# Hybrid decoder layer: attention products in one array shape, split values, a longer lag, and the FFN's token sums on VectorE

## The chip, the core and the metric

The kernel runs on one core of a Trainium2 chip. The metric is the device time of one execution in microseconds (us). The core's engines are named as the profile names them: PE (TensorE's matmuls), PEld (its weight loads), DVE (VectorE), ACT (ScalarE), POOL (GpSimd) and SP, which issues the transfers. Each engine takes its instructions in a fixed order, and they wait for each other through semaphores.

## What is computed

One layer, 512 tokens, width 1024, float32. Three groups of heads share one input projection: six attention heads of 64 channels, a state-space mixer (SSD) and a pooling mixer. Their outputs are joined, projected and added to the input; a gated feed-forward part (FFN) and a last norm follow. Attention selects three blocks of 256 keys, but with 512 tokens there are only two blocks, so it is plain causal attention:

```python
h = rmsnorm(x, norm_mix)
q, k, v, z, xbc, dt_raw, p_in = jnp.split(h @ w_in, offsets, axis=-1)
p = softmax(q @ k.T * 64 ** -0.5 + causal)        # per head, 512 tokens
y_attn = p @ v
y_ssd = ssd_mixer(xbc, z, dt_raw, ...)            # chunks of 128 tokens, gated norm
y_pool = pool_mixer(p_in, pool_w, pool_scale)
x = x + concatenate([y_attn, y_ssd, y_pool]) @ w_out
gate, up = split(rmsnorm(x, norm_ffn) @ w_gate_up)
x = x + (silu(gate) * up) @ w_down
out = rmsnorm(x, norm_final)
```

## The kernel before

**Precision.** Large products are done in float32r on split operands: a value is a high part (rounded by ACT, `AF.Copy` into a float32r tile) and a low part (value minus high part, on DVE or POOL). `mm3` (lines 163 to 168) makes three products of them: high by high, high by low, low by high. Plain float32 products appear too; the trace shows each of those as two rows on PE.

**Stages.** First come the projections: `proj_nat` makes token-major tiles (`pn`: v, and z with dt), `proj_ch` channel-major ones (`pc`: q, k, the conv inputs, the pool input). While they run, small jobs are woven in: attention, SSD, pooling. Then the output projection (`po`, in two halves of columns), then the boundary: each of four token tiles gets its residual (`add_x1`), its norm (`h2_norm`, tile `xh`), a transposition (`h2_bank`, tile `ps_h`) and its split into `h2_hi` and `h2_lo`. The FFN multiplies by a seven-product (Strassen-like) scheme, so it needs sums and differences of token tiles as well: `h2_sums` makes t1 to t4 for token tiles 2 and 3, splits each, and writes them to `T2`, `T3`, `T4` and `h2`. Then the gate and up products (`psf`) and the down products (`pd`, `pdl`).

**Attention.** `evac_v` writes v (`v_sb`, float32). `evac_q` and `evac_k` make, for each pair of heads j (three pairs), `qa` and `qb`: in the own 64 partitions the high part of q, in the other 64 the low part; `ka` and `kb`: the high part of k in both; `kl`: the low parts of both heads, 64 partitions each, made on POOL. `scores` (576 to 593) then needs two products for 128 tokens of queries: q by k over all 128 partitions, and high q by low k over the head's own 64 (line 584). DVE adds the mask and takes the row minimum (589), ACT takes the exponential and its sum (590), DVE the reciprocal (591) and the scaling (592). `probs_t` (595) transposes the probabilities on PE and copies them to SBUF, on ACT for the first head of a pair and DVE for the second. `values` (609 to 614) multiplies v by them in float32, into 64 of the 128 output partitions:

```python
nc.tensor.matmul(ps_o[hd, i * P : (i + 1) * P], v_sb[:, b, col], pt[:, b * P : (b + 1) * P], ...)
```

A step is one head and one tile i of 128 queries, 24 in all, in the order pair, tile, head. `attention_lane` gives out scores of step n, transposes of step n-1, values of step n-2.

**What sets the order.** Lanes (generators) are resumed by a clock that counts the PE time given out so far (`L.tick`, `L.clock`), with delays in the tables `ATT`, `SSD` and marks such as `mark("dt", 9.0)`. A scheduler then places each engine's instructions by its own model when the program is built. `ENG` (line 48) says for token tiles 2 and 3 which of five subtractions of `h2_sums` go to DVE (v) and to POOL (g): in order t3, and the low parts of t2, t3, t1 and t4.

## Time and profile before

| | us |
|---|---|
| median of 3 runs (lowest to highest) | 597.58 (596.22 to 598.58) |
| the profiled execution | 597.45 |
| its span, from the first to the last instruction | 595.7 |
| PE busy | 576.7 (97%) |
| DVE busy | 458.1 (77%) |
| ACT busy | 272.9 (46%) |
| POOL busy | 65.3 (11%) |
| granted TensorE clock, mean of the span | 0.99 |

PE's busy time counts overlapping matmuls once, and the end of a matmul is modelled, so what a matmul costs its neighbours is read from the start of one row to the start of the next. The clock is given as a share of the higher of its two levels (2.4 GHz): 1.00 is that level, 0.50 the lower one (1.2 GHz).

### The profile page before, as it was taken

Reading aid. Unit: us, or ns where it says so; the run is one execution under the profiler, and the core shown is the slowest. Engines: PE = TensorE matmul, PEld = TensorE weight load, DVE = VectorE, ACT = ScalarE, POOL = GpSimd, SP = SyncE. Lnnn points to the kernel's source line nnn. Section 1 sums busy time; section 2 is a strip of 40 time slices with the busy share of each in tenths; the row PEclk is TensorE's granted clock in tenths of the full one; section 3 lists DMA queues with packets and bytes.
Section 4 is the critical chain, followed back from the end, with each engine's and each line's share of the span. In section 5 each row is a group of like instructions: output and inputs, shape, how many; then the busy total and the mean of one; then the engine's idle time right before and its main releaser. Section 6 shows DMA issues by size and latency. Waiting matters only on the chain.

```text
span 595.7 us, 9142 instructions
## 1 busy us (share of the span) xinstructions
PE 576.7 (97%) x3540; PEld 505.9 (85%) x3540; DVE 458.1 (77%) x815; ACT 272.9 (46%) x459; POOL 65.3 (11%) x78
## 2 busy tenths in 40 slices
PE   8998999999999999799999999999999999999994
PEld 5995698777876787799889988999899989999984
DVE  4487558596897757999999987798869977888445
ACT  5674434664553546536525541554144523325135
POOL 5020000201953010500000000000000000000024
PEclk9998999999999999899999999999999999999998
DMA  7952124221221450033623431243224424212003
GB/s 240 308 171 72 35 72 141 96 102 56 70 72 36 137 216 2 36 109 110 206 72 108 146 103 70 77 173 107 70 72 142 139 75 142 72 53 90 2 0 142
DMA packets 19520, 61.64 MB, mean 103 GB/s; under 512 B 2300, under 2 KB 3476, under 8 KB 19476
## 3 DMA queue, kind: packets, MB, share of 16 engines
q1 hardware_dynamic: 19476, 61.05, 30.7%
q8 instruction: 28, 0.46, 0.3%
q14 instruction: 16, 0.13, 0.1%
HBM read 58.93 MB, written 2.11 MB: 102 GB/s over the span
## 4 chain that ended last, share of the span: by engine, by line
PE 89%; DVE 6%; ACT 2%; issue 1%; DMA 1%; SPq 0%; DVEq 0%; ACTq 0%
PE psf L164 11%; PE psf L165 11%; PE psf L166 11%; PE pd L164 6%; PE pd L165 6%; PE pd L166 6%; PE pc L164 5%; PE pc L165 4%; PE pc L166 4%; PE po L164 2%; PE po L165 2%; PE po L166 2%; PE ps_ao L613 2%; PE pn L164 2%; PE pn L166 2%; PE pn L165 2%
## 5 line engine op out<-in xcount | busy, mean ns | idle before, releaser
L165 PE MATMUL pd<-dl,aTh 128*128 128x512 f32 x160 | 63.3, 395 | 0.0
L164 PE MATMUL pd<-dh,aTh 128*128 128x512 f32 x160 | 62.6, 395 | 0.0
L166 PE MATMUL pd<-dh,aTl 128*128 128x512 f32 x160 | 60.0, 395 | 0.0
L1032 DVE TENSOR_TENSOR E<-psf,E 128x256 f32<-128x256 f32 x110 | 42.1, 418 | 11.2 <-PE psf L166 10.3
L164 PE MATMUL psf<-h_hi,gh 128*128 128x256 f32 x176 | 49.9, 285 | 0.1
L165 PE MATMUL psf<-h_lo,gh 128*128 128x256 f32 x176 | 49.7, 283 | 0.0
L165 PE MATMUL psf<-h_lo,sh 128*128 128x256 f32 x176 | 49.7, 282 | 0.0
L166 PE MATMUL psf<-h_hi,gl 128*128 128x256 f32 x176 | 49.7, 283 | 0.0
L166 PE MATMUL psf<-h_hi,sl 128*128 128x256 f32 x176 | 49.5, 281 | 0.0
L164 PE MATMUL psf<-h_hi,sh 128*128 128x256 f32 x176 | 49.5, 281 | 0.0
L136 DVE TENSOR_TENSOR wlo<-raw,whi 128x1024 fp32r<-128x1024 f32 (+3 forms) x29 | 33.2, 1144 | 18.8 <-ACT whi L135 16.1
L135 ACT ACTIVATE whi<-raw 128x1024 fp32r<-128x1024 f32 (+3 forms) x34 | 31.6, 932 | 34.1 <-PE pc L165 19.2
L164 PE MATMUL pc<-hT_hi,whi 128*128 128x512 f32 x104 | 43.2, 415 | 0.0
L165 PE MATMUL pc<-hT_lo,whi 128*128 128x512 f32 x104 | 41.5, 399 | 0.0
L166 PE MATMUL pc<-hT_hi,wlo 128*128 128x512 f32 x104 | 41.4, 398 | 0.0
L1124 POOL TENSOR_TENSOR x<-x,gf 128x512 f32<-128x512 f32 x4 | 5.1, 1299 | 322.6 <-ACT sqf L747 322.6
L782 ACT ACTIVATE dh<-r_d 128x1024 fp32r<-128x1024 f32 x22 | 23.0, 1055 | 33.8 <-PE psf L165 22.5
L782 ACT ACTIVATE sh<-sb 128x1024 fp32r<-128x1024 f32 x22 | 23.2, 1057 | 32.8 <-PE pd L165 26.0
L783 DVE TENSOR_TENSOR sl<-sb,sh 128x1024 fp32r<-128x1024 f32 x22 | 28.0, 1271 | 13.3 <-ACT sh L782 9.6
L166 PEld LDWEIGHTS pd<-dh,aTl 128*128 128x128 f32 x160 | 30.1, 188 | 7.2
L739 DVE TENSOR_TENSOR x<-pd,x 128x512 f32<-128x512 f32 x44 | 28.3, 685 | 10.1 <-PE pd L166 10.1
L164 PEld LDWEIGHTS pd<-dh,aTh 128*128 128x128 f32 x160 | 30.1, 188 | 7.0
(286 smaller groups left out, 1706.3 us busy)
## 6 DMA issues: line engine op xcount, KB each, us to landing
r_g<-wgu SPq DMA_DIRECT2D x22, 512.0 KB, 3.8
r_u<-wgu SPq DMA_DIRECT2D x22, 512.0 KB, 4.1
r_d<-wd SPq DMA_DIRECT2D x22, 512.0 KB, 3.3
raw<-w SPq DMA_DIRECT2D x13, 512.0 KB, 3.3
raw<-wo SPq DMA_DIRECT2D x8, 512.0 KB, 3.2
rawx<-xT SPq DMA_DIRECT2D x8, 256.0 KB, 3.5
rawn<-xn SPq DMA_DIRECT2D x4, 512.0 KB, 4.7
x<-xn SPq DMA_DIRECT2D x4, 512.0 KB, 6.6
```

What stands on the lines that cost most here:

```text
L135: nc.scalar.activation(hi[:, sl], raw[:, sl], AF.Copy)
L136: eng.tensor_tensor(lo[:, sl], raw[:, sl], hi[:, sl].bitcast(F32), ALU.subtract)
L164: nc.tensor.matmul(ps, s_hi, m_hi, start=first, stop=False)
L165: nc.tensor.matmul(ps, s_hi, m_lo, start=False, stop=False)
L166: nc.tensor.matmul(ps, s_lo, m_hi, start=False, stop=last)
L613: nc.tensor.matmul(ps_o[hd, i * P : (i + 1) * P], v_sb[:, b, col], pt[:, b * P : (b + 1) * P], start=(b == 0), stop=(b == i))
L739: nc.vector.tensor_tensor(x1[t][:, cs], ps, x1[t][:, cs], ALU.add)
L782: nc.scalar.activation(hi, src, AF.Copy)
L783: eng.tensor_tensor(lo, src, hi.bitcast(F32), ALU.subtract)
L1032: nc.vector.tensor_tensor(o_, a_, b_, ALU.add)
L1124: nc.gpsimd.tensor_tensor(x1[t][:, :512], x1[t][:, :512], gf[0][:, :512], ALU.mult)
```

## The change

Attention: `evac_v` now splits v into a high part (ACT) and a low part (DVE), side by side in one tile of 128 columns for each head (`v_hl`). The low part of k gets one tile for each head, with zeros in the other 64 partitions (set once on POOL), so that both score products run over 128 partitions. `probs_t` splits the transposed probabilities into `ph` (ACT) and `pl` (DVE) for two query tiles in one tile of 256 columns. `values` multiplies `v_hl` by `ph` and by `pl` in float32r, for two query tiles at a time: the output has the products with the high part of v in one half of the partitions and those with the low part in the other. `attention_out` copies one half across (ACT), adds the halves (DVE), and splits the sum after the second head. The steps now run pair, head, tile; transposes follow their scores by two steps, and values their transposes by two more. The delays of two lanes are longer. `ENG` sends all five subtractions of both token tiles to DVE. The smaller scratch for dynamic DMA frees memory.

```diff
--- before.py
+++ after.py
@@ -41,11 +41,13 @@
 VFIRST = (1, 2, 2, 3)
 WARM = 10
 ATT = (1.2, 0.4, 0.4)
+ATT_LAG = 2
+VAL_LAG = 2
 SSD = (3.0, 3.0, 1.5)
 LAST = 256
 NDEC = 4
 NW = 6
-ENG = ("vggvg", "vvgvg")
+ENG = ("vvvvv", "vvvvv")
 MIX_ORDER = (0, 6, 1, 7, 3, 4, 5, 2)
@@ -270,7 +272,7 @@
         rstd_bc = mp.tile([P, S], F32, name="rstd_bc")
         def norm_lane():
-            yield 20.0
+            yield 23.0
             ps = bank("ps_rstd")
             for t in range(NT):
                 nc.tensor.matmul(ps[:, t * P : (t + 1) * P], rstd[:, t : t + 1].to_broadcast([P, P]), ident, start=True, stop=True)
@@ -347,7 +349,7 @@
             nc.vector.scalar_tensor_tensor(sz[:, t], th, 1.0, sz[:, t], ALU.add, ALU.mult)
             if t == NT - 1:
                 softplus()
-                mark("dt", 9.0)
+                mark("dt", 13.0)
         def softplus():
             nc.scalar.activation(s_, dtr, AF.Abs)
@@ -536,11 +538,17 @@
-        v_sb = mp.tile([P, NT, 384], F32, name="v_sb")
+        v_hl = mp.tile([P, NT, NH, P], F32R, name="v_hl")
+        kl_sb = [mp.tile([P, S], F32R, name=f"kl{h}") for h in range(2)]
         qk_sb = {}
         def evac_v(t, ps):
-            nc.vector.tensor_scalar_mul(v_sb[:, t], ps[:, :384], rstd[:, t : t + 1])
+            src, hi, lo = h3(ps[:, :384]), v_hl[:, t, :, :64], v_hl[:, t, :, 64:]
+            nc.scalar.activation(hi, src, AF.Copy, scale=rstd[:, t : t + 1])
+            nc.vector.scalar_tensor_tensor(lo, src, rstd[:, t : t + 1], hi.bitcast(F32), ALU.mult, ALU.subtract)
             if t == NT - 1:
                 mark("v", 4.0)
@@ -564,9 +572,10 @@
             def f(ps):
                 k = w2k(f"k{j}")
                 nc.vector.tensor_tensor(k, ps, rstd_bc, ALU.mult)
-                kl = qk_tile("kl", j)
-                for name, own, other in (("ka", H0, H1), ("kb", H1, H0)):
+                for name, kl, own, other in (("ka", kl_sb[0], H0, H1), ("kb", kl_sb[1], H1, H0)):
                     t_ = qk_tile(name, j)
+                    if j == 0:
+                        nc.gpsimd.memset(kl[other].bitcast(F32), 0.0)
                     nc.scalar.activation(t_[own], k[own], AF.Copy)
                     nc.scalar.activation(t_[other], k[own], AF.Copy)
                     nc.gpsimd.tensor_tensor(kl[own], k[own], t_[own].bitcast(F32), ALU.subtract)
@@ -575,13 +584,12 @@
         def scores(j, i, h):
             n = (i + 1) * P
-            hd = (H0, H1)[h]
             nm = f"{j}{i}{h}"
             ps = bank(f"ps_s{nm}")
-            q, k, kl = qk_sb["qa" if h == 0 else "qb", j], qk_sb["ka" if h == 0 else "kb", j], qk_sb["kl", j]
+            q, k, kl = qk_sb["qa" if h == 0 else "qb", j], qk_sb["ka" if h == 0 else "kb", j], kl_sb[h]
             qs = slice(i * P, (i + 1) * P)
             nc.tensor.matmul(ps[:, :n], q[:, qs], k[:, :n], start=True, stop=False)
-            nc.tensor.matmul(ps[:, :n], q[hd, qs], kl[hd, :n], start=False, stop=True)
+            nc.tensor.matmul(ps[:, :n], q[:, qs], kl[:, :n], start=False, stop=True)
             L.clock += 2 * max(0.109, n * 0.00042)
             pr = w2k(f"pr{nm}")
             mn = tiny.tile([P, 1], F32, name=f"mn{nm}", tag="mn")
@@ -592,46 +600,65 @@
             nc.vector.tensor_scalar_mul(pr[:, :n], pr[:, :n], sm)
             return pr
-        def probs_t(j, i, h, pr):
+        def probs_t(j, i, h, pr, pt):
             n = (i + 1) * P
             nm = f"{j}{i}{h}"
             ps_t = bank(f"ps_t{nm}")
             for b in range(i + 1):
                 nc.tensor.transpose(ps_t[:, b * P : (b + 1) * P], pr[:, b * P : (b + 1) * P], ident)
             L.clock += 0.11 * (i + 1)
-            pt = w2k(f"pt{nm}")
-            if h == 0:
-                nc.scalar.copy(pt[:, :n], ps_t[:, :n])
-            else:
-                nc.vector.tensor_copy(pt[:, :n], ps_t[:, :n])
-            return pt
+            hi, lo = (x_[:, : i + 1, (i % 2) * P : (i % 2 + 1) * P] for x_ in pt)
+            src = ps_t[:, :n].rearrange("p (b q) -> p b q", q=P)
+            nc.scalar.activation(hi, src, AF.Copy)
+            nc.vector.tensor_tensor(lo, src, hi.bitcast(F32), ALU.subtract)
         def values(j, i, h, pt, ps_o):
-            hd = slice(64 * h, 64 * h + 64)
-            col = slice(128 * j + 64 * h, 128 * j + 64 * h + 64)
             for b in range(i + 1):
-                nc.tensor.matmul(ps_o[hd, i * P : (i + 1) * P], v_sb[:, b, col], pt[:, b * P : (b + 1) * P], start=(b == 0), stop=(b == i))
-            L.clock += 0.22 * (i + 1)
+                q0 = P if b == i else 0
+                w_ = v_hl[:, b, 2 * j + h]
+                o_ = ps_o[:, (i - 1) * P + q0 : (i + 1) * P]
+                for x_ in pt:
+                    nc.tensor.matmul(o_, w_, x_[:, b, q0:], start=(b == 0 and x_ is pt[0]), stop=(b == i and x_ is pt[1]))
+                    L.clock += 0.109 if b < i else 0.07
+        def attention_out(j, h, ps_o, y):
+            own, other = (H0, H1) if h == 0 else (H1, H0)
+            aux = w2k(f"aux{j}{h}")
+            nc.scalar.copy(aux[own], ps_o[other])
+            nc.vector.tensor_tensor(y[own], ps_o[own], aux[own], ALU.add)
+            if h == 1:
+                nc.scalar.activation(mixT_hi[:, j], y, AF.Copy)
+                nc.vector.tensor_tensor(mixT_lo[:, j], y, mixT_hi[:, j].bitcast(F32), ALU.subtract)
+                mark(f"mix{j}", 3.5)
         def attention_lane():
-            steps = [(j, i, h) for j in range(3) for i in range(NT) for h in range(2)]
-            pr, pt, outs = {}, {}, {}
-            for n in range(len(steps) + 2):
+            steps = [(j, i, h) for j in range(3) for h in range(2) for i in range(NT)]
+            pr, pt, outs, ys = {}, {}, {}, {}
+            for n in range(len(steps) + ATT_LAG + VAL_LAG):
                 if n < len(steps):
-                    if steps[n][1:] == (0, 0):
-                        yield when("v", f"k{steps[n][0]}")
-                    pr[n] = scores(*steps[n])
+                    j, i, h = steps[n]
+                    if (i, h) == (0, 0):
+                        yield when("v", f"k{j}")
+                    pr[n] = scores(j, i, h)
                     yield ATT[0]
-                if 1 <= n <= len(steps):
-                    pt[n - 1] = probs_t(*steps[n - 1], pr.pop(n - 1))
+                m = n - ATT_LAG
+                if 0 <= m < len(steps):
+                    j, i, h = steps[m]
+                    if i % 2 == 0:
+                        pt[j, h, i // 2] = [wk.tile([P, NT, 256], F32R, name=f"p{x_}{j}{h}{i}", tag=f"p{x_}") for x_ in "hl"]
+                    probs_t(j, i, h, pr.pop(m), pt[j, h, i // 2])
                     yield ATT[1]
-                if n >= 2:
-                    j, i, h = steps[n - 2]
-                    if (i, h) == (0, 0):
-                        outs[j] = bank(f"ps_ao{j}")
-                    values(j, i, h, pt.pop(n - 2), outs[j])
-                    if (i, h) == (NT - 1, 1):
-                        mix_out(j, outs.pop(j))
+                m -= VAL_LAG
+                if m >= 0 and steps[m][1] % 2:
+                    j, i, h = steps[m]
+                    if i == 1:
+                        outs[j, h] = bank(f"ps_ao{j}{h}")
+                    values(j, i, h, pt.pop((j, h, i // 2)), outs[j, h])
+                    if i == 3:
+                        if h == 0:
+                            ys[j] = w2k(f"y{j}")
+                        attention_out(j, h, outs.pop((j, h)), ys[j])
                     yield ATT[2]
@@ -1211,7 +1238,7 @@
     import concourse.bacc as bacc
     from concourse.bass_utils import run_bass_kernel_spmd as run
-    nc = bacc.Bacc("TRN2", target_bir_lowering=False, num_devices=1)
+    nc = bacc.Bacc("TRN2", target_bir_lowering=False, num_devices=1, dynamic_dma_scratch_size=1024)
     arrays, args = {}, []
     for name, a in pack(inputs).items():
         a = np.ascontiguousarray(a)
```

On PE, at the first steps of attention (`ps_s` scores, `ps_t` transposes, `ps_ao` values, `pc` a projection), there stands before:

```order
L166 MATMUL pc_506<-hT_hi,wlo_361 128x512
L600 MATMUL ps_t_529<-ident,pr_482 128x128
L583 MATMUL ps_s_536<-ka_440,qa_431 128x256
L584 MATMUL ps_s_536<-kl_439,qa_431 128x256
L600 MATMUL ps_t_552<-ident,pr_516 128x128
L613 MATMUL ps_ao_559<-pt_531,v_sb 64x128
L164 MATMUL pc_578<-hT_hi,whi_396 128x512
```

The transpose of the second step's probabilities (`pr_516`) stands right behind the scores of the third. In the changed kernel the first step's transpose stands so:

```order
L168 MATMUL pc_513<-hT_hi,wlo_363 128x512
L608 MATMUL ps_t_554<-ident,pr_489 128x128
L591 MATMUL ps_s_561<-ka_445,qa_437 128x512
L592 MATMUL ps_s_561<-kl_243,qa_437 128x512
L166 MATMUL pc_591<-hT_hi,whi_392 128x512
```

The fourth step's scores (512 columns) stand behind it, where the second step's transpose stood. That one (`pr_523`) comes after the 24 rows of projection `pc_591`, again on PE:

```order
L168 MATMUL pc_591<-hT_hi,wlo_393 128x512
L608 MATMUL ps_t_595<-ident,pr_523 128x128 x2
L591 MATMUL ps_s_603<-kb_450,qb_440 128x128
L592 MATMUL ps_s_603<-kl_244,qb_440 128x128
L489 MATMUL ps_bn_613<-ident,bc_234 128x128 x4
L608 MATMUL ps_t_627<-ident,pr_539 128x128 x3
```

The first values have moved behind the fourth step's transposes.

On PE, at the end of attention, the transposes of the SSD output (`ps_sn`) stand behind this in the changed kernel (`ps_t_1939` is the last step's transpose, `po` the output projection):

```order
L608 MATMUL ps_t_1939<-ident,pr_1862 128x128 x4
L622 MATMUL ps_ao_1949<-ph_1850,v_hl 128x256
L622 MATMUL ps_ao_1949<-pl_1851,v_hl 128x256
L622 MATMUL ps_ao_1949<-ph_1850,v_hl 128x128
L622 MATMUL ps_ao_1949<-pl_1851,v_hl 128x128
L168 MATMUL po_0_1788<-whi_1463,mixT_lo 128x512
L168 MATMUL po_1_1789<-whi_1463,mixT_lo 128x512
L168 MATMUL po_2_1790<-whi_1463,mixT_lo 128x512
L168 MATMUL po_3_1791<-whi_1463,mixT_lo 128x512
L533 MATMUL ps_sn_1991<-ident,sz 128x128
L533 MATMUL ps_sn_1998<-ident,sz 128x128
```

Between the last SSD product (`ps_y`) and the first of these `ps_sn` rows PE now has 13 rows of `po`, 10 transposes, two scores of 512 columns, one pool product (two rows of 512 columns) and 11 value products; before, the first `ps_sn` came behind much more of `po` and of the values.

On DVE, at the boundary, between the sums of token tile 2 and the norm of token tile 3 (`xh`), there stands before:

```order
L947 SCALAR_TENSOR_TENSOR tf_2315<-tf_2313,h2f_2223 128x512
L936 TENSOR_TENSOR h_lo<-tf_2312,h_hi 128x4x128
L759 TENSOR_SCALAR rsaa_2331<-rsay_2330,rsav_2328 128x1
L760 TENSOR_SCALAR rsay_2330<-rsaa_2331,rsay_2330 128x1
L905 SCALAR_TENSOR_TENSOR xh_2337<-x_3_2009,rsay_2330,gn 128x512 x2
```

and in the changed kernel:

```order
L974 SCALAR_TENSOR_TENSOR tf_2380<-tf_2378,h2f_2288 128x512
L786 TENSOR_SCALAR rsaa_2396<-rsay_2395,rsav_2393 128x1
L963 TENSOR_TENSOR h_lo<-tf_2377,h_hi 128x4x128
L963 TENSOR_TENSOR T3l<-tf_2379,T3h 128x4x128
L963 TENSOR_TENSOR T2l<-tf_2378,T2h 128x4x128
L787 TENSOR_SCALAR rsay_2395<-rsaa_2396,rsay_2395 128x1
L963 TENSOR_TENSOR T4l<-tf_2380,T4h 128x4x128
L932 SCALAR_TENSOR_TENSOR xh_2402<-x_3_2074,rsay_2395,gn 128x512 x2
```

Three subtractions of 128 by 512 that stood on POOL now stand ahead of `xh` on DVE. For token tile 3 two more follow.

## Rows read from the trace of the kernel before

**Rows 1.** The profile's page: busy time of each engine with its share of the span, and the chain of work that ended last, by engine.

```profile
PE 576.7 (97%) x3540; PEld 505.9 (85%) x3540; DVE 458.1 (77%) x815; ACT 272.9 (46%) x459; POOL 65.3 (11%) x78
...
PE 89%; DVE 6%; ACT 2%; issue 1%; DMA 1%; SPq 0%; DVEq 0%; ACTq 0%
```

**Rows 2.** The view by stretches: start and end, length, then busy us (and instructions) of PE, PEld, DVE, ACT and POOL, the granted clock, the DMA share and GB/s. The stretch in which most of attention runs, and the fifth of it in which DVE is fullest.

```profile
100.00:200.00 100.00, 99.41 (x523) 76.91 (x522) 77.00 (x183) 51.83 (x124) 33.72 (x41) 1.00 0.21 70
160.00:180.00 20.00, 20.00 (x110) 15.46 (x109) 19.35 (x43) 11.05 (x34) 13.07 (x20) 1.00 0.23 73
```

**Rows 3.** The timeline of PE (start, duration, line, operation, tiles, array shape, columns), two pairs of score products.

```profile
54.52 0.28 PE L583 MATMUL ps_s<-kb,qb 128*128 128x256 f32 x1
54.73 0.38 PE L584 MATMUL ps_s<-kl,qb 64*128 64x256 f32 x1
...
145.38 0.48 PE L583 MATMUL ps_s<-kb,qb 128*128 128x512 f32 x1
145.79 0.50 PE L584 MATMUL ps_s<-kl,qb 64*128 64x512 f32 x1
```

**Rows 4.** The chain of waits in order of time (start, the time it takes on the chain, what), 45 to 82 us: score products of 128, 256 and 512 columns, and runs of value rows.

```profile
45.90 0.25 PE ps_s L584
46.59 0.06 PE ps_s L583
...
54.69 0.12 PE ps_s L583
54.80 0.31 PE ps_s L584
...
60.30 0.36 PE ps_ao L613 x2
...
63.70 0.58 PE ps_ao L613 x4
...
73.23 0.23 PE ps_s L583
73.47 0.43 PE ps_s L584
...
77.30 0.80 PE ps_ao L613 x6
```

**Rows 5.** The instructions of lines 584 and 613: how many, duration in ns (least, median, most), first and last start in us, array shape and columns.

```profile
L584 PE MATMUL ps_s<-kl,qa x12: 323/410/501, 45.8 to 189.0; 64*128 64x128 f32 x3, 64*128 64x256 f32 x3, 64*128 64x384 f32 x3, 64*128 64x512 f32 x3
L584 PE MATMUL ps_s<-kl,qb x12: 323/408/498, 47.3 to 192.2; 64*128 64x128 f32 x3, 64*128 64x256 f32 x3, 64*128 64x384 f32 x3, 64*128 64x512 f32 x3
...
L613 PE MATMUL ps_ao<-pt,v_sb x120: 272/273/324, 53.3 to 202.3; 128*64 128x128 f32 x120
```

**Rows 6.** The timeline of PE at the second step's transpose; in brackets the idle time before it and what ended it.

```profile
53.09 0.33 PE L600 MATMUL ps_t<-ident,pr 128*128 128x128 f32 x1 [2.86 <-DVE pr L592]
```

**Rows 7.** The view by stretches (columns as in Rows 2): that wait, the stretch of low clock after it, and the one at the boundary.

```profile
50.20:53.10 2.90, 0.04 (x2) 0.02 (x1) 2.78 (x11) 1.99 (x7) 0.00 (x0) 1.00 0.21 38
...
55.10:58.40 3.30, 3.30 (x9) 2.62 (x9) 2.61 (x6) 0.84 (x3) 0.00 (x0) 0.50 0.00 0
...
246.30:249.60 3.30, 2.71 (x13) 2.74 (x14) 2.56 (x5) 1.91 (x4) 0.00 (x0) 0.50 0.41 156
```

**Rows 8.** Groups of instructions, 40 to 206 us (count, busy us, mean ns of one, then idle time before them): the copies of the probabilities on DVE and ACT, and between them a low part of 512 columns from PSUM on DVE.

```profile
L606 DVE COPY pt<-ps_t 128x128 f32<-128x128 f32 (+3 forms) x12 | 5.8, 487 | 5.7 <-PE ps_t L600 5.7
L297 DVE TENSOR_TENSOR mixT_lo<-ps_ao,mixT_hi 128x512 fp32r<-128x512 f32 x3 | 2.0, 682 | 0.0
...
L604 ACT COPY pt<-ps_t 128x128 f32<-128x128 f32 (+3 forms) x12 | 5.0, 414 | 3.7 <-PE ps_t L600 3.7
```

**Rows 9.** The timelines of PE and DVE, 177 to 197 us: the last SSD product, the start of the SSD norm, its last scaling, and the first transposes of the result.

```profile
177.41 1.45 PE L461 MATMUL ps_y<-xdt,dec 128*128 128x64 f32 x12
...
182.59 0.17 DVE L521 TENSOR_SCALAR ssq<-ssq 128x8 f32<-128x8 f32 x1 [2.27 <-ACT jy L472]
...
192.10 0.54 DVE L526 TENSOR_SCALAR sz<-sz,rs_y 128x192 f32<-128x192 f32 x2
...
196.11 0.60 PE L531 MATMUL ps_sn<-ident,sz 128*128 128x128 f32 x4
```

**Rows 10.** The timelines of DVE, POOL and PE at the boundary.

```profile
232.69 1.42 DVE L905 SCALAR_TENSOR_TENSOR xh<-x,rsay,gn 128x512 f32<-128x512 f32 x2 [0.35 <-PE ps_h L912]
...
241.63 1.77 DVE L936 TENSOR_TENSOR h_lo<-tf,h_hi 128x512 fp32r<-128x512 f32 x1
...
243.88 2.87 DVE L905 SCALAR_TENSOR_TENSOR xh<-x,rsay,gn 128x512 f32<-128x512 f32 x2
...
249.89 0.69 DVE L936 TENSOR_TENSOR h_lo<-tf,h_hi 128x512 fp32r<-128x512 f32 x1
250.49 2.32 DVE L783 TENSOR_TENSOR sl<-sb,sh 128x1024 fp32r<-128x1024 f32 x1
...
260.38 1.22 DVE L783 TENSOR_TENSOR sl<-sb,sh 128x1024 fp32r<-128x1024 f32 x1
...
242.82 1.71 POOL L936 TENSOR_TENSOR T2l<-tf,T2h 128x512 fp32r<-128x512 f32 x1
...
245.22 0.63 PE L912 MATMUL ps_h<-ident,xh 128*128 128x128 f32 x4 [2.95 <-DVE xh L905]
246.89 1.09 PE L912 MATMUL ps_h<-ident,xh 128*128 128x128 f32 x4 [1.05 <-DVE xh L905]
```

## Prediction, made before the changed kernel ran

> **What bounds the kernel now.** I read the page first. PE is busy 97% of the span, the next engine (DVE) 77%, and 89% of the chain that ended last is PE's [rows 1]. So the time is PE's time, and a change counts for what it takes from PE's queue or what it makes PE wait. Next I read the stretches: from 100 to 200 us, where most of attention runs, PE is busy 99.41 of 100 us and DVE 77.0, and between 160 and 180 DVE has 19.35 of 20 [rows 2]. PE is the bound there, with DVE close behind. Since a busy PE may still be slow, I then read what attention's matmuls cost from start to start [rows 3, 4]. Two full-shape score products of 256 columns would take 0.12 us each; the one over 64 partitions takes 0.31. Last I looked for where PE stands still: 2.86 us at 53 us, behind the scaling on DVE [rows 6], and twice at the boundary, 2.95 and 1.05 us, behind the norm of token tile 3 [rows 10].
>
> **The change part by part**, against the profiled execution (597.45 us: the span of 595.7 and 1.75 around it; the median of the runs is 597.58, so no correction is due).
>
> *Scores in one shape.* On the chain a product over 64 partitions takes 0.25, 0.31 and 0.43 us for 128, 256 and 512 columns, one over 128 partitions 0.06, 0.12 and 0.23 [rows 4]. The difference is 0.19 to 0.20 at every size, so it is no matter of columns but a price for leaving the shape: 24 such products [rows 5] x 0.195 = 4.7 us. Entering it costs as well: the full-shape product ahead starts 0.21 us before the other at 256 columns (0.12 alone, so 0.09) and 0.41 at 512 (0.23, so 0.18) [rows 3, 4]. That is 24 x 0.09 to 0.18 = 2.2 to 4.3. The new product streams as many columns over 128 partitions and costs what the first of the pair costs. I take 8.5 of 6.9 to 9.0: the upper entry price, a little less. Gain 8.5.
>
> *Values.* A run of two, four and six value rows takes 0.36, 0.58 and 0.80 us [rows 4]: 0.11 for a row and 0.14 on top for the end of the run. With 120 rows [rows 5], in 23 runs (counted in the timeline, the first at 53.3 and the last at 202.3), this is 13.2 + 3.2, and entering the narrow shape costs 0.09 at the least, as above, 2.1 more: 18.5. The new form has, for each of six heads, eight products of 256 columns and four of 128: 48 x 0.12 + 24 x 0.06 = 7.2 us by the float32r scores of those sizes [rows 4]; if the short ones cost as much as a value row, 0.11, it is 8.4. Gain 11.0, between 10.1 and 11.3.
>
> *The wait at 53 us.* PE stands 2.86 us while DVE is busy 2.78 of 2.90, and from 55.1 to 58.4 the granted clock is 0.50 with PE busy all through [rows 6, 7], which costs half of 3.3, 1.65. With the lag of two the second step's transpose stands behind 24 projection rows, 5.5 us of PE work. On DVE more is queued ahead of it: two more mask rows, of 384 and 512 columns. I keep 0.5 for what is left of the wait; 0 if DVE is in time, 2.9 if nothing is won. Gain 4.5 before that.
>
> *The token sums on DVE.* POOL's subtractions slow DVE while they run: `h_lo` takes 1.77 us beside POOL and 0.69 alone, two `xh` halves 2.87 and 1.42, the 1024-column low part 2.32 and 1.22 [rows 10]. For token tile 3, `xh` now has three subtractions ahead of it (3 x 0.69 = 2.1), gets 1.1 back on `h_lo`, so it starts 1.0 later, and its two halves take 0.7 each. The first half is ready 0.3 later, the second 0.4 earlier, and PE needs both. What PE wins is 0.4, and perhaps as much after 250 us, where DVE gets 2.2 back for two more subtractions (1.4) but PE hardly waits. I take 1.0. It could be a loss of 1, if the speed of DVE beside POOL is not the reason for its slow rows; if `xh` came so early that half of the waits and of the low clock behind them went (2.95 + 1.05 + 1.65 us, [rows 7, 10]), 3.
>
> *More work beside PE.* Twelve copies of probabilities on DVE (5.8 us) become 24 subtractions, twelve on ACT (5.0) become 24 [rows 8]; six sums of halves, at 0.68 by the low part of 512 columns from PSUM [rows 8], are 4.1 more on DVE. So DVE gets 9.9 us. The six copies across and the four high parts of v come on ACT, which is busy 51.83 of 100 us where attention is thickest [rows 2]; for DVE the low parts of v replace the scalings of v. The cover of this is PE's time: 100 to 200 us has 23 us free on DVE. Two of three head pairs fall there. The change takes two thirds of 19.5, 13 us, of PE's time from it and adds two thirds of 9.9, 6.6, to DVE: 83.6 of 87 us, 96%. DVE still fits, without slack. While DVE is held up by what POOL does (13.07 of 20 us from 160 to 180, [rows 2]), PE's transposes, which stand behind the scaling, will wait now and then: 0 to 3, I take 1.5.
>
> *The SSD norm.* From the end of the last SSD product (178.86 us) to the last scaling (192.64) the chain over POOL, ACT and DVE takes 13.8 us, and PE reaches the transposes only at 196.11, so it was hidden [rows 9]. Now PE has 13 rows of 0.23, ten transposes and eleven value products of at most 0.12, two scores of 0.23 and the pool product (two float32 rows of 512 columns, estimated at twice 0.23 each): some 6.5 us, and 0.9 more to the last transpose. The chain's own part is shorter than 13.8, since DVE waited in it for attention's products. If it takes 13.8, PE waits 6.4; if it takes 7.4, nothing. I take the middle, 3.0.
>
> *The small edits.* The longer lane delays and the zeroing of two tiles on POOL at the start, where POOL has nothing else but constants to set, cost nothing that PE sees. The transfers keep their order but for the SSD's decay tiles among the loads of `wo`, far ahead of use.
>
> Sum: 597.45 - 8.5 - 11.0 - 4.5 - 1.0 + 0.5 + 1.5 + 3.0 = 577.45, about **577 us**.
>
> **The rivals.** (A) *DVE becomes the bound of attention.* For: 96% of its time is booked, it has a queue in fixed order, and it waits for products of PE and exponentials of ACT in between; before, 97% was reached only over 20 us [rows 2]. Against: before and after that stretch DVE has room, and PE's queue carries projections between scores and transposes. If DVE runs at 85%, the 83.6 us take 98.4 instead of 87: 11.4 in the place of the 4.5 that I put in for two waits, 584 us; with a low clock or two behind such waits, 588. The Trainium skill (TensorEngine Tiling (Array Packing), Performance Considerations) warns that a faster TensorE can leave the evacuation of PSUM as the bottleneck, which is this case.
>
> (B) *The transposes wait for their softmax, step by step* (slower than before). If the longer lag does not suffice, each of the 24 steps can stand as PE stood at 53 us: 2.86 us and 1.65 for the clock, 4.5. The gains are 25.0, so from six such waits on the change loses; with eight it is 597.45 - 25.0 + 36 = 608. For: the rows of DVE ahead of each scaling grow. Against: one step in 24 waited before, with a lag of one, and one step's own rows take under 3 us.
>
> (C) *The shape is not what costs.* If the 0.195 and 0.14 belong to something that stays, such as a group's last product, the gains of shape (8.5, and 5.3 of the values) don't come: 577 + 13.8 = 591. For: no row shows a lone change of shape without a new group. Against: a full-shape score inside a projection costs 0.06 [rows 4], and it starts a group as well.
>
> (D) *Narrow shapes are worth having.* If the 64-partition products cost less than full ones, widening them costs what they save, at most their streaming: 24 x 0.15 = 3.6 us instead of 8.5 won, 577 + 12.1 = 589. Every pair read says the contrary [rows 3, 4], and no two narrow products run side by side. The Trainium skill (TensorEngine Tiling (Array Packing), Overview, Theoretical Speedup) states such a rule: up to twice the speed where a dimension is at most 64.
>
> **How the numbers follow.** The forecast has 0.69, (A) 0.21, (B) 0.04, (C) 0.05, (D) 0.01. The forecast's own range: no new waits give 577.45 - 5.0 = 572.5, half of the boundary's waits another 2 less, 570; with the wait at 53 us kept, the SSD norm's 6.4 and 3 of the others it is 585. Range 569 to 587, which takes in most of (A). A measurement of this kernel can tell a change of about 0.5%, 3 us, from none: faster means under 594.6. The forecast, (A) but for a tail, (C) and (D) are faster: 0.94; 0.03 the same; (B) but for a small part, slower: 0.03.
>
> **What would show it.** No row on PE may have a shape other than 128 by 128 but for the one narrow product of the decay sums; score products should start 0.06 to 0.23 apart, values 0.12 and 0.06. The wait at 53 us and the low clock behind it should be gone or under 1 us. DVE should be over 90% busy in attention. A wait of PE before the `ps_sn` rows of some 3 us would show the SSD norm uncovered. At the boundary two waits of PE should remain, the second shorter, and DVE's 2.87 should be 1.4. The prediction is wrong if PE waits in many steps for the scaling (B), or if the value rows start 0.2 us apart.

## The result, and the profile after

The changed kernel takes 577.25 us (median of 4 runs, 576.24 to 578.24), the kernel before 597.62 in the same series: 0.9661 of it, with a 95% interval of 0.9634 to 0.9688. The forecast was 577. The profiled execution took 577.72 us, its span is 576.0.

The page: busy time of each engine, and the chain that ended last, by engine.

```profile
PE 557.9 (97%) x3492; PEld 501.6 (87%) x3492; DVE 463.0 (80%) x838; ACT 281.0 (49%) x481; POOL 60.1 (10%) x75
...
PE 61%; DVE 7%; ACT 1%; issue 1%; DVEq 0%; ACTq 0%
```

PE lost 18.8 us of busy time and is still 97% busy, so it still sets the time [rows 1]. DVE gained 4.9, POOL lost 5.2. The chain is followed back only to 174 us here, so its shares add up to 70% and are not to be set against those of before.

The waits of PE (line that waited, releaser, us in total, how often, the longest):

```profile
PE ps_h L939 <- DVE xh L932: 3.7, 2, 2.8
...
PE po L166 <- ACT mixT_hi L301: 1.5, 1, 1.5
...
PE ps_pool L700 <- DVE y L629: 0.6, 1, 0.6
PE ps_t L608 <- DVE sk L469: 0.4, 1, 0.4
PE po L166 <- DVE yo L467: 0.4, 1, 0.4
PE ps_t L608 <- DVE mn L597: 0.2, 1, 0.2
```

The wait for the scaling (`pr`) at 53 us [rows 6] is gone. In its place stand five waits between 156 and 177 us (`mixT_hi`, `y`, `sk`, `yo`, `mn`), 3.1 us together. The view by stretches (start and end, length, busy us of PE, PEld, DVE, ACT and POOL, granted clock, DMA share, GB/s): the first half of attention, most of it, the part with the five waits, and the stretch behind the boundary's wait.

```profile
40.00:60.00 20.00, 20.00 (x101) 16.63 (x100) 16.90 (x36) 13.38 (x25) 3.58 (x5) 1.00 0.31 93
100.00:183.00 83.00, 79.69 (x451) 66.78 (x450) 75.88 (x178) 51.99 (x131) 32.42 (x38) 1.00 0.22 71
140.00:180.00 40.00, 36.80 (x210) 30.16 (x209) 36.30 (x94) 22.57 (x64) 26.66 (x31) 1.00 0.18 60
...
226.70:230.00 3.30, 3.30 (x16) 3.29 (x17) 2.27 (x4) 1.44 (x3) 0.00 (x0) 0.50 0.45 144
```

From 40 to 60 us PE never stands and the clock stays at 1.00 [rows 7 had 0.50 there]. From 100 us to the end of attention DVE is 91% busy (75.88 of 83). The low clock behind the boundary's wait is still there.

The timeline of PE: a pair of score products of 384 columns behind value rows, value rows of 256 and 128 columns, a pair of 512 behind a transposition.

```profile
62.65 0.39 PE L591 MATMUL ps_s<-kb,qb 128*128 128x384 f32 x1
62.87 0.33 PE L592 MATMUL ps_s<-kl,qb 128*128 128x384 f32 x1
63.05 0.28 PE L622 MATMUL ps_ao<-ph,v_hl 128*128 128x256 f32 x1
...
64.34 0.28 PE L622 MATMUL ps_ao<-pl,v_hl 128*128 128x256 f32 x1
64.46 0.22 PE L622 MATMUL ps_ao<-ph,v_hl 128*128 128x128 f32 x1
64.52 0.28 PE L622 MATMUL ps_ao<-pl,v_hl 128*128 128x128 f32 x1
64.62 0.30 PE L608 MATMUL ps_t<-ident,pr 128*128 128x128 f32 x1
64.68 0.48 PE L591 MATMUL ps_s<-kb,qb 128*128 128x512 f32 x1
65.00 0.39 PE L592 MATMUL ps_s<-kl,qb 128*128 128x512 f32 x1
65.23 0.38 PE L608 MATMUL ps_t<-ident,pr 128*128 128x128 f32 x2
```

Values start 0.12 and 0.06 apart (the last short one of a run 0.10 ahead of the transposition), the second score product ends its turn after 0.18 (384 columns) and 0.23 (512). Every shape is 128 by 128. The *first* product of a pair still takes more than its columns ask for: 0.32 at 512, where 0.23 is usual. The transposition ahead of it shows 0.06 instead of its 0.11, so part of this is only where a row's start is recorded; keep it in mind for the term on scores.

The boundary: the rows of DVE ahead of the norm of token tile 3, and PE's two waits there [rows 10].

```profile
225.24 0.68 DVE L963 TENSOR_TENSOR T4l<-tf,T4h 128x512 fp32r<-128x512 f32 x1
225.84 1.41 DVE L932 SCALAR_TENSOR_TENSOR xh<-x,rsay,gn 128x512 f32<-128x512 f32 x2
```

```profile
218.21 1.32 PE L939 MATMUL ps_h<-ident,xh 128*128 128x128 f32 x8 [0.85 <-DVE xh L932]
226.64 1.97 PE L939 MATMUL ps_h<-ident,xh 128*128 128x128 f32 x8 [2.85 <-DVE xh L932]
```

`xh` takes 1.41 us for both halves (2.87 before), and the wait for its second half, 1.05 before, is gone; the wait for the first half is 2.85 (2.95 before).

### The profile page after: what moved, and what is told of

The parts are those of the page before. It is cut to its first block, busy times and chain, and to the rows that moved or that the text cites. A ratio compares the mean times of both kernels' runs of the same rounds, so it can differ in the third digit from the quotient of the medians.

```text
span 576.0 us, 9083 instructions
## 1 busy us (share of the span) xinstructions
PE 557.9 (97%) x3492; PEld 501.6 (87%) x3492; DVE 463.0 (80%) x838; ACT 281.0 (49%) x481; POOL 60.1 (10%) x75
## 4 chain that ended last, share of the span: by engine, by line
PE 61%; DVE 7%; ACT 1%; issue 1%; DVEq 0%; ACTq 0%
PE psf L166 12%; PE psf L168 11%; PE psf L167 11%; PE pd L166 6%; PE pd L167 6%; PE pd L168 6%; PE po L166 2%; PE po L167 2%; PE po L168 2%; PE ps_h L939 1%; DVE sl L810 1%; DVE E L1059 1%; DVE x L1169 0%; DVE sz L528 0%; ACT sqf L1172 0%
## 5 line engine op out<-in xcount | busy, mean ns | idle before, releaser
L1059 DVE TENSOR_TENSOR E<-psf,E 128x256 f32<-128x256 f32 x110 | 42.4, 418 | 11.2 <-PE psf L168 10.3
L166 PE MATMUL pc<-hT_hi,whi 128*128 128x512 f32 x104 | 41.3, 397 | 0.0
L167 PEld LDWEIGHTS pd<-dl,aTh 128*128 128x128 f32 x160 | 30.1, 188 | 6.9
```

What stands on the lines that cost most here:

```text
L166: nc.tensor.matmul(ps, s_hi, m_hi, start=first, stop=False)
L167: nc.tensor.matmul(ps, s_hi, m_lo, start=False, stop=False)
L1059: nc.vector.tensor_tensor(o_, a_, b_, ALU.add)
```

## The experiments

Four series, each with runs of the kernel before on the same chip; what is compared is the ratio to that kernel. The changed kernel's own ratio, 0.9661, was taken in another series and its interval is 0.0027 to either side, so a difference under some 1.6 us between an experiment and the changed kernel says nothing by itself; there the rows decide. One per cent is 6 us.

**narrow_scores** puts the low score product back on 64 partitions.

```diff
+hd = (H0, H1)[h]
...
-nc.tensor.matmul(ps[:, :n], q[:, qs], kl[:, :n], start=False, stop=True)
+nc.tensor.matmul(ps[:, :n], q[hd, qs], kl[hd, :n], start=False, stop=True)
```

> The changed kernel with one edit: the low score product runs over the head's own 64 partitions again (the other 64 hold zeros, so the sum is the same). The steps' order, the lag and the split values stay. Theory (leaving the narrow shape costs 0.195 us, entering it 0.09 to 0.18, 24 times): 6.9 to 9.0 longer than the changed kernel's 577.25, so 584 to 586, and each score product over 64 partitions takes 0.25, 0.31 and 0.43 for 128, 256 and 512 columns again. Rival C (the price belongs to the end of a group, not to the shape): 577, and the rows keep their length. Rival D (narrow products are worth having): 573.6.

Measured: 582.05 us, ratio 0.9749 (0.9730 to 0.9767), so 5.3 us more than the changed kernel. PE's timeline shows the pair of 384 columns in the same place as above, and the one of 512:

```profile
63.43 0.39 PE L592 MATMUL ps_s<-kb,qb 128*128 128x384 f32 x1
63.74 0.43 PE L593 MATMUL ps_s<-kl,qb 64*128 64x384 f32 x1
64.11 0.39 PE L623 MATMUL ps_ao<-ph,v_hl 128*128 128x256 f32 x1
...
65.86 0.47 PE L592 MATMUL ps_s<-kb,qb 128*128 128x512 f32 x1
66.26 0.49 PE L593 MATMUL ps_s<-kl,qb 64*128 64x512 f32 x1
66.68 0.44 PE L609 MATMUL ps_t<-ident,pr 128*128 128x128 f32 x2
```

Set against the changed kernel's: 0.31 instead of 0.22 on entering (384), 0.40 instead of 0.32 (512), 0.37 instead of 0.18 and 0.42 instead of 0.23 on leaving. Leaving costs 0.19, entering 0.08 to 0.09 at both sizes. The row behind the product is longer too: 0.22 (64.11 to 64.33) where the changed kernel has 0.11 (63.05 to 63.16). Products that follow one another share these ends, so in PE's whole timeline the rows next to the 24 products come to 7.0 us more, 0.29 each. Rivals C and D are out for the scores. That the time is 5.3 longer and not 7.0 is for the most part PE's waits: `mixT_hi`, `yo` and `mn` have 1.8 us here and all five waits 3.1 in the changed kernel.

**scores_alone** gives the kernel before the two zero-padded tiles of low parts, and with them both score products over 128 partitions; the rest stays.

```diff
-nc.tensor.matmul(ps[:, :n], q[hd, qs], kl[hd, :n], start=False, stop=True)
+nc.tensor.matmul(ps[:, :n], q[:, qs], kl[:, :n], start=False, stop=True)
```

> The kernel before with the scores alone in one shape: one tile of low parts of k for each head with zeros in the other 64 partitions, both score products over 128 partitions. Nothing else moves but what the order follows. Undoing this in the changed kernel cost some 5.6 us. Theory (the price of the shape is paid on PE, and PE is the bound of attention before and after): 5.5 to 7 less than before, 0.988 to 0.991. Rival (in the kernel before the gain is lost in its wait at 53 us or in others): 0.995 or above.

Measured: 592.01 us, ratio 0.9887 (0.9856 to 0.9917): 6.7 us less than before, though PE still waits at 54 us, longer than before (3.4 us for `pr`). The gain of the shape needs nothing else of the change.

**narrow_values** takes the value products in 64 of 128 columns, in float32r; it leaves out the products with the low part of v.

```diff
-w_ = v_hl[:, b, 2 * j + h]
-o_ = ps_o[:, (i - 1) * P + q0 : (i + 1) * P]
+w_ = v_hl[:, b, 2 * j + h, :64]
+o_ = ps_o[H0, (i - 1) * P + q0 : (i + 1) * P]
...
-nc.scalar.copy(aux[own], ps_o[other])
-nc.vector.tensor_tensor(y[own], ps_o[own], aux[own], ALU.add)
+nc.scalar.copy(aux[own], ps_o[H0])
+nc.vector.tensor_tensor(y[own], aux[own], aux[own], ALU.add)
```

> The changed kernel with the value products in 64 of the 128 columns of the array: their number and their columns stay (72 rows of 256 or 128 columns), but the products with the low part of v are left out, and the sum of halves on DVE adds the copied half to itself. Only the array shape of the value rows changes. They stand in 18 runs in PE's order. Theory (0.09 for entering and 0.14 to 0.20 for the end of a run): 18 x 0.23 to 0.29 = 4.1 to 5.2 longer than 577.25, so 581.4 to 582.5. Rival C (the 0.14 belongs to the end of a run, whatever its shape): 577. Rival D: the narrow rows run faster, under 577.

Measured: 582.07 us, ratio 0.9742 (0.9719 to 0.9764), 4.8 more than the changed kernel: the size that was expected. But the rows do not bear it out:

```profile
62.29 0.39 PE L168 MATMUL pc<-hT_hi,wlo 128*128 128x512 f32 x1
62.52 0.28 PE L622 MATMUL ps_ao<-pl,v_hl 128*64 128x256 f32 x1
...
63.17 0.23 PE L622 MATMUL ps_ao<-pl,v_hl 128*64 128x128 f32 x1
63.23 0.29 PE L608 MATMUL ps_t<-ident,pr 128*128 128x128 f32 x1
```

The projection row ahead takes 0.23 from start to start, as it always does, and the last value row 0.06, as in the full shape: entering and leaving cost nothing. What made the time longer are waits: 3.1 us in three waits of transposes for `pr`, 1.8 for the scaled SSD output ahead of `ps_sn`. The edited sum of halves on DVE reads two operands in SBUF instead of one in PSUM and takes up to 1.45 us (0.69 in the changed kernel); that this alone moved DVE so far is not shown. So a right size was found for a wrong reason, and the rows, not the time, are the verdict: in float32r this narrow shape has no price.

**float_wide** and **float_narrow** take the value products as plain float32, in the full shape and (with the edit of narrow_values) in 64 columns.

```diff
-nc.tensor.matmul(o_, w_, x_[:, b, q0:], ...)
+nc.tensor.matmul(o_, w_.bitcast(F32), x_[:, b, q0:].bitcast(F32), ...)
```

> The changed kernel with the value products taken as plain float32 instead of float32r, in the full shape, on the same split values: 72 rows, all over 128 by 128. Each row should take twice as long from start to start (0.22 for 256 columns, 0.11 for 128): 48 x 0.10 + 24 x 0.05 = 6.0 more, and nothing for entering or leaving, since transposes in float32 of the full shape cost their neighbours nothing: 577.25 + 6.0 = 583.2, or some 0.7 less, as the kernel before measured 0.9 less in the last series. If the price at the ends of the value runs of the kernel before belongs to float32 and not to the shape, the 18 runs cost 0.19 each on top here as well, 3.4: 586.6.

> The kernel of narrow_values (value products in 64 of the 128 columns, the low part of v left out) in plain float32 instead of float32r. narrow_values showed no price at either end of a run of value rows, where the kernel before shows 0.09 at each. Theory (the price belongs to float32 in the narrow shape): the rows next to the value runs show 0.09 on entering and 0.09 on leaving here, 18 times each, 3.3 us more than float_wide in the sum over the rows' starts. Rival (it belongs to using both halves of the columns in turn, which the kernel before does and this one doesn't): none here. The time itself hangs on new waits as well (narrow_values had some), so the rows decide: 585 to 592.

Measured: 590.07 us, ratio 0.9874 (0.9853 to 0.9895), and 594.85, ratio 0.9968 (0.9952 to 0.9983). PE's timelines, first the full shape, then the narrow one (x2: a product is two rows):

```profile
61.05 0.39 PE L167 MATMUL pc<-hT_lo,whi 128*128 128x512 f32 x1
61.28 0.59 PE L622 MATMUL ps_ao<-pl,v_hl 128*128 128x256 f32 x2
61.71 0.38 PE L622 MATMUL ps_ao<-ph,v_hl 128*128 128x128 f32 x2
61.93 0.39 PE L622 MATMUL ps_ao<-pl,v_hl 128*128 128x128 f32 x2
62.07 0.42 PE L591 MATMUL ps_s<-kb,qb 128*128 128x384 f32 x1
```

```profile
62.30 0.39 PE L167 MATMUL pc<-hT_lo,whi 128*128 128x512 f32 x1
62.62 0.65 PE L622 MATMUL ps_ao<-pl,v_hl 128*64 128x256 f32 x2
63.10 0.38 PE L622 MATMUL ps_ao<-ph,v_hl 128*64 128x128 f32 x2
63.32 0.38 PE L622 MATMUL ps_ao<-pl,v_hl 128*64 128x128 f32 x2
63.63 0.45 PE L591 MATMUL ps_s<-kb,qb 128*128 128x384 f32 x1
```

A product of 256 columns takes 0.43 in float32, not the 0.22 that the expectation used: it forgot that there are two rows of 0.22. By these lengths float_wide is 48 x 0.31 + 24 x 0.16 = 18.7 dearer; 12.7 were measured. The single lengths overstate it: from the first score product to the last row of the output projection, all rows of PE, from start to start, come to 15.8 us more than in the changed kernel. PE, slower now, waits 2.6 less there, which leaves 13.2.

In the full shape the row ahead keeps its 0.23. In the narrow one it takes 0.32, the first product 0.48 instead of 0.43, and the last, in the same place, 0.31 instead of 0.14: 0.31 more for this run. The theory of this pair holds: the price belongs to float32 in 64 columns. But it is larger than the 0.09 at each end that the expectation took from the kernel before: float_narrow takes 5.6 us more than float_wide by the ratios, and 3.3 were expected. The rival (two halves in turn) is out, since only one half is used here.

**lag_one** sets both lags of the changed kernel to one, **lag_alone** gives the kernel before a lag of two for the transposes.

```diff
-ATT_LAG = 2
-VAL_LAG = 2
+ATT_LAG = 1
+VAL_LAG = 1
```

```diff
-if 1 <= n <= len(steps):
-    pt[n - 1] = probs_t(*steps[n - 1], pr.pop(n - 1))
+if 2 <= n <= len(steps) + 1:
+    pt[n - 2] = probs_t(*steps[n - 2], pr.pop(n - 2))
...
-    values(j, i, h, pt.pop(n - 2), outs[j])
+    values(j, i, h, pt.pop(n - 3), outs[j])
```

> The changed kernel with both lags at one: transposes follow their scores by one step, values their transposes by one. Theory (the lag of two is what took the wait at 53 us and its low clock away): that wait comes back, 2.9 us and 1.65 for the clock, and with more queued on DVE other steps wait a little too: 581 to 585. Rival (the wait went because steps now run head by head, the lag does nothing): 577. Rival B's premise (each step waits for its own softmax when the lag is short): six waits or more, 600 and above.

> The kernel before with the lag alone: transposes follow their scores by two steps instead of one, values their transposes by one as before; the products, their shapes and everything else stay. By the prediction's term (the wait at 53 us and its half clock gone, 0.5 left): 4.0 to 4.5 less than before, 0.992 to 0.993 of its time, and no wait of PE over 1 us between 45 and 60 us. Rival (in the kernel before the wait is no matter of the lag; it moves to the next step): 1.000.

lag_one measured 599.91 us, ratio 1.0054 (1.0035 to 1.0072): 23.5 more than the changed kernel, and slower than the kernel before. Its waits of PE:

```profile
PE ps_t L608 <- DVE pr L600: 13.5, 5, 5.8
PE ps_t L608 <- DVE sm L599: 4.4, 1, 4.4
...
PE ps_ao L622 <- DVE pl L613: 2.1, 1, 2.1
```

Six waits of transposes and one of values, 20.0 us, and behind two of the longest the clock is at its lower level (stretches as above):

```profile
53.00:57.00 4.00, 4.00 (x11) 3.23 (x12) 2.86 (x8) 1.91 (x4) 0.10 (x1) 0.50 0.02 4
...
124.50:129.00 4.50, 4.36 (x14) 3.58 (x15) 3.81 (x8) 2.15 (x6) 0.10 (x1) 0.50 0.00 0
```

lag_alone measured 594.76 us, ratio 0.9965 (0.9950 to 0.9979): 2.1 less than before, half of the term. The wait at 53 us is gone, as the term said; but a new one stands at 114.66, behind the convolution of the SSD's input, which DVE now reaches later (PE's timeline):

```profile
114.66 0.66 PE L478 MATMUL ps_xn<-ident,xs 128*128 128x128 f32 x4 [1.55 <-DVE xs L386]
```

So the lag is not a gain of 4.5 beside the others. With a lag of one the new products and splits would have lost all that they won.

**sums_back** undoes the table of engines for the token sums.

```diff
-ENG = ("vvvvv", "vvvvv")
+ENG = ("vggvg", "vvgvg")
```

> The changed kernel with the table of engines for the token sums as before: three of the five subtractions for token tile 2 and two for token tile 3 are on POOL again. By the prediction's term: 1.0 longer than the changed kernel (between 3 longer and 1 shorter), 578.2; rows of DVE beside POOL's take 1.4 to 2.3 where they take 0.7 to 1.2 now, and a wait of PE for the second half of the norm of token tile 3 comes back (1 us). Rival (the norm waits for fewer rows on DVE, so it is earlier): 1 to 2 shorter.

Measured: 577.96 us, ratio 0.9682 (0.9663 to 0.9701), 1.3 more than the changed kernel, inside what the two intervals allow. The traces agree on the size: from the last row of the output projection to the end of the span it takes 361.1 us here, 359.9 in the changed kernel and 361.2 in the kernel before. The rows show the mechanism: beside POOL's subtractions DVE takes twice as long, and PE waits for the second half again (timelines of DVE and PE).

```profile
223.05 1.58 DVE L963 TENSOR_TENSOR h_lo<-tf,h_hi 128x512 fp32r<-128x512 f32 x1
...
224.79 3.19 DVE L932 SCALAR_TENSOR_TENSOR xh<-x,rsay,gn 128x512 f32<-128x512 f32 x2
```

```profile
228.12 1.08 PE L939 MATMUL ps_h<-ident,xh 128*128 128x128 f32 x4 [0.66 <-DVE xh L932]
```

**norm_first** turns DVE's order at the boundary: `h2_norm` of token tile 3 ahead of the subtractions and the fourth sum of token tile 2.

```diff
+with tc.issue_after(xh_ins[3]):
     return eng.tensor_tensor(dst[n][1], f_, dst[n][0].bitcast(F32), ALU.subtract)
...
+with tc.issue_after(xh_ins[3]):
     nc.vector.scalar_tensor_tensor(t4, t2, -1.0, b21, ALU.mult, ALU.subtract)
```

> The changed kernel with DVE's order at the boundary turned: the norm of token tile 3 (its last scaling writes xh) stands ahead of four subtractions and the fourth sum of token tile 2, not behind them. Nothing is added or left out. In the changed kernel PE waits 2.85 us at 223.8 for this xh, and the clock is at its lower level for 3.3 us behind the wait. Theory (the wait is DVE's queue, not the norm's own chain): xh starts about 3 us earlier, the wait shrinks to under 0.5 and the low clock goes with it: 2.4 to 4.5 less, 572.8 to 574.9. Rival (DVE is the bound from 219 to 248 us, since its rows follow one another without a gap there, and the order changes nothing in their sum): what PE wins at 224 it waits for later, 577.

Measured: 575.44 us, ratio 0.9638 (0.9620 to 0.9656): the lowest of all, 1.4 less than the changed kernel, with overlapping intervals. DVE's and PE's timelines:

```profile
221.57 1.42 DVE L934 SCALAR_TENSOR_TENSOR xh<-x,rsay,gn 128x512 f32<-128x512 f32 x2
...
231.25 0.69 DVE L966 TENSOR_TENSOR T2l<-tf,T2h 128x512 fp32r<-128x512 f32 x1
```

```profile
231.99 0.39 PE L167 MATMUL psf<-T2l,sh 128*128 128x256 f32 x1 [1.50 <-DVE T2l L966]
```

`xh` no longer stands behind the subtractions; the wait of 2.85 and the low clock behind it (4.5 us together) are gone. But DVE has no gap from 217 to 236 us, the low parts come no earlier than its rows allow, and PE waits 1.5 for `T2l` and 0.7 for a weight's low part later. From the last row of the output projection to the end it takes 358.9 us, 1.0 less than the changed kernel. Both the theory and the rival are half right: the wait was DVE's queue, and the queue as a whole binds.

**scale_act** moves the scaling of 16 of 24 steps to ACT, **norm_scale** joins it with norm_first.

```diff
-nc.vector.tensor_scalar_mul(pr[:, :n], pr[:, :n], sm)
+if j == 0:
+    nc.vector.tensor_scalar_mul(pr[:, :n], pr[:, :n], sm)
+else:
+    nc.scalar.activation(pr[:, :n], pr[:, :n], AF.Copy, scale=sm)
```

> The changed kernel with the scaling of the probabilities of head pairs 2 and 3 (16 of 24 steps) on ACT instead of DVE; nothing is left out. In the changed kernel PE waits some 4 us in five places between 155 and 177 us, each time for a row of DVE, or of ACT behind one of DVE, while DVE is busy 36.3 of the 40 us from 140 to 180 and ACT 22.6. The edit takes some 7.7 us of rows off DVE there and gives ACT about 8. Theory (DVE's queue is what PE waits for there, the mild form of rival A): 2 to 4 shorter than the changed kernel, which stands at 0.966 of the kernel before: 0.960 to 0.963. Rival (the waits are the length of the chain over POOL, ACT and DVE, and ACT's queue takes the place of DVE's): 0.966 or above, with the wait for the pool mixer's high part (1.5 us) unchanged or longer.

> norm_first and scale_act together: the norm of token tile 3 ahead of the sums of tile 2 on DVE, and the scaling of pairs 2 and 3 on ACT. The two places lie 40 us apart, so the gains should add: norm_first measured 0.9638 of the kernel before (the changed kernel 0.9661), and with 2 to 4 us from scale_act this would be 0.957 to 0.961. If scale_act gives nothing, 0.964.

Measured: 576.97 us, ratio 0.9644 (0.9615 to 0.9673), and 578.47, ratio 0.9665 (0.9639 to 0.9692): neither can be told from the changed kernel. DVE is relieved, from 75.88 to 68.62 of the 83 us up to 183, and yet PE's waits up to there are longer in the profiled executions, 5.1 us instead of 3.1 (scale_act's two largest; its profiled execution, 579.40 us, is the longest of its five):

```profile
PE po L166 <- ACT mixT_hi L301: 2.5, 2, 1.8
PE ps_t L611 <- ACT pr L603: 2.3, 2, 1.8
```

They are now waits for ACT. The rival holds, and DVE's busy share alone is not what PE waits for; whether it is the length of the chain over several engines or ACT's queue in DVE's place, this run does not part. norm_scale has the same 5.1 us of waits in attention, 2.0 more than norm_first, which covers the 1.6 us that it lies behind it.

**pool_early** moves the two projections of the pool mixer ahead of those of q and k of the third pair of heads.

```diff
+for j in range(2):
+    proj_ch(U_P + j, evac_p(j))
+    L.add(pool_lane(j))
 proj_ch(U_Q2, evac_q(2))
 proj_ch(U_Q2 + 1, evac_k(2))
-for j in range(2):
-    proj_ch(U_P + j, evac_p(j))
-    L.add(pool_lane(j))
```

> The changed kernel with the two projections of the pool mixer ahead of those of q and k of the third pair of heads, not behind them; their weights are loaded in that order too. Nothing is left out. scale_act took rows off DVE and the waits of PE between 155 and 183 us stayed. Theory (PE runs short of other work there: it waits for the ends of three chains, the pool mixer's, the SSD's and the last attention steps', that all come late): the pool mixer's and the SSD's chains end some 10 us earlier, their waits (0.6, 0.4 and 1.5 us) go and output projections stand between the last attention steps: 2 to 3 less than the changed kernel's 0.966, so 0.961 to 0.963. Rival (the third pair's chain of 24 steps becomes the end of everything, as it starts 11 us later and too little is left for PE beside it): waits of PE for pr and pl in the last eight steps, 0.970 or above.

Measured: 591.19 us, ratio 0.9884 (0.9850 to 0.9918), 13.3 more. The pool mixer's product itself now waits 4.3 us for its input, the output projection 2.3 for attention's sum, and the boundary 6.3 instead of 3.7; behind the wait of 4.3 the clock reads 0.51 for 3.3 us. The rival's direction is right, its mechanism only in part, since the longest wait is the pool mixer's own.

## Why the prediction was right, and where its terms were not

| term | forecast | measured | from |
|---|---|---|---|
| scores in one shape | -8.5 | -6.7 | scores_alone; 5.3 by narrow_scores, 7.0 by its rows |
| values | -11.0 | -10.3 | some 17 for both products, less 6.7 (below) |
| wait and clock at 53 us | -4.5 + 0.5 | -4.5 | no wait of PE from 40 to 60 us |
| token sums on DVE | -1.0 | -1.3 | sums_back (not clear of noise) |
| more work beside PE | +1.5 | +3.1 | the five waits |
| SSD norm uncovered | +3.0 | 0 | no wait before `ps_sn` |
| sum | -20.0 | -19.7 | profiled 577.72 - 597.45 = -19.7 |

The direction and the main mechanisms are as forecast. That the total is right to 0.3 us is luck, because the misses cancel: 2.5 too much gain on PE's products and 1.6 too little for the new waits, against 3.0 for a wait that did not come and 0.8 in the two terms between.

The two products together are measured: from the first score product to the last row of the output projection the changed kernel takes 173.05 us (43.05 to 216.10), the kernel before 191.70 (42.87 to 234.57). That is 18.65 less, with 3.3 us of idle PE in place of 3.5, and 1.65 of it is the low clock; some 17 are left for both. How they divide is an estimate, good to about half a us.

**Scores.** The mechanism is as forecast: a price for leaving the shape that does not depend on the columns. The term that was mis-sized is the entry, 0.09 to 0.18. The 0.41 read at 512 columns stood behind a transposition, where a full-shape product takes 0.32 as well; entering is 0.09 at every size. The longer row behind was in no term. The low end, 6.9, is near what the rows add up to, 7.0.

**Values.** The forecast took 13.2 for the rows, 0.14 on top of a run and 0.09 for entering. In the rows of the kernel before, the row ahead of a run is 0.09 longer, its first row 0.05 (0.16 instead of 0.11) and its last 0.09 (0.20), so these prices hold; the 0.14 is both ends and not the end alone, and the row behind, up to 0.11 longer as well, was not counted. What was mis-sized is the new form: from start to start its 72 rows take 8.5 us, not 7.2 (the forecast's own upper figure was 8.4), in part because the last short row of most runs takes 0.10 to 0.11 instead of 0.06. 18.5 - 8.5 is 10.0, near the 10.3 that are left. What the forecast had wrong is the cause: it put the ends down to the shape. float_narrow and narrow_values say that it takes float32 *and* 64 columns; in float32r the narrow form would have cost nothing at its ends. The gain of the values comes from float32r (0.12 instead of 0.43 for 256 columns) and not from the array's shape, which in the new form is merely where the high and low parts of v stand side by side. So rival C was half right here: for the values, shape alone is not what costs. Whether float32 makes a difference in 64 rows as well, no run here shows.

The Trainium skill (TensorEngine Tiling (Array Packing), Key Properties) says that a change of the tiling mode drains TensorE; its list of modes (Available Configurations) has 64 of 128 rows and 64 of 128 columns alike, and no price or number format beside them. The rows agree for 64 rows (0.29 a product) and for 64 columns in float32 (0.31 for the run shown), and disagree for 64 columns in float32r (0). Whether the last form is a mode of its own at all, the traces don't say.

**The wait at 53 us.** Gone as forecast, with its low clock. As a separate gain the term is misleading. lag_alone won 2.1 of it in the kernel before, where another wait took its place. lag_one shows what the lag is for in the changed kernel: without it PE waits 20.0 us. That is rival B's mechanism, priced 4.5 a step and here 2.9 (20.0 in seven waits) and the clock; the forecast's reason against it, that one step's rows take under 3 us and only one step in 24 waited, did not hold for a short lag. It was the longer lags (lag_one shortens both at once) that kept B away.

**Token sums.** By its own steps: `xh` at 1.4, the second wait gone. The forecast expected the first to grow by 0.3; it went from 2.95 to 2.85.

**More work beside PE, and the SSD norm.** The forecast booked DVE at 96% and had 1.5 for it; DVE is at 91%, and the waits cost 3.1. The SSD norm was to cost 3.0 ahead of `ps_sn`; PE does not wait there, though the norm's last scaling ends at 180.75 and the first `ps_sn` starts at 180.14, with nothing to spare. The likely reason is that it had stood 1.5 us at 174.8 for the pool mixer's high part. I read these two terms as one: late chains over POOL, ACT and DVE end between 156 and 183 us, and PE, 17 us faster, comes to them with little else to do. Together 4.5 were forecast, 3.1 came. narrow_values, where `ps_sn` waits 1.8 and others 3.1, shows the same place in another order. Rival A named the engine (DVE); with 7.3 us of DVE's rows gone in scale_act the waits did not shrink.

**Which chain to shorten** stays open: pool_early made one of them earlier and lost 13 us on others.

## What to carry to other kernels

Read the price of an array shape at its edges, from the start of the row ahead to the start of the row behind, and separately for each number format: 64 rows in float32r and 64 columns in float32 cost some 0.3 us for each visit here, 64 columns in float32r nothing. Count the row ahead, the first and the last row, and the row behind. When the bound engine becomes faster, the lag between dependent steps has to grow with it: the same new products are 3.4% faster than before with a lag of two and 0.5% slower with a lag of one. An experiment's time can land on the expected number for another reason; the rows at the edit decide.

## What the runs showed of the hardware that was not expected

- Value products in 64 of 128 columns start like full-shape ones in float32r (0.23 ahead of them, 0.06 for the last), but in float32 the run shown cost 0.31: 0.09 on the row ahead, 0.05 on the first product and 0.17 on the last.
- A float32 product of 256 columns takes 0.43 us in two rows, a float32r one 0.12: a factor of 3.6.
- DVE's norm of 2 x 512 columns took 1.41 us alone, 2.87 and 3.19 beside POOL's subtractions.
- The length of a wait alone does not say what the clock does behind it. Waits of PE of 2.85 us (changed kernel, at 223.8), 4.44 and 5.82 (lag_one, before 52.90 and 124.64) and 4.26 (pool_early) were followed by the lower level (0.50 to 0.51) for 3.3 us or more with PE busy. Behind one of 2.64 in lag_one (before 73.75) the clock reads 0.62 over 3.3 us, but behind one of 2.90 in the same run (before 198.57) 1.00. Behind the wait of 1.75 at the start of the changed kernel it reads 0.72 from 7 to 13 us; behind those of 1.5 in norm_first (232 us) and lag_alone (114.7) 1.00.
